# Layer-norm statistics on another engine in a hybrid decoder trunk: ScalarE's accumulators in place of VectorE's batch-norm instructions

## The chip, the core and the metric

The kernel runs on one core of a Trainium2 chip. A core has TensorE (PE, matmuls and transpositions; PEld is its weight load), VectorE (DVE), ScalarE (ACT), GpSimd (POOL) and SyncE (SP, which here only issues DMAs). Each engine works through its own queue in order; semaphores let an instruction wait for another engine or for a DMA. The metric is the device time of one execution in microseconds; of several executions the median is taken.

## The reference

One decoder layer on 1024 positions of 1024 features. The normalised input is projected to four parts; three mixers work on them, one of which is the spatial gating unit that this change touches:

```
h = rms_norm(x, g_mix)
z_a, z_b, z_u, z_v = split(h @ w_in)            # 384, 256, 384, 384 columns
y_a = s5_mixer(z_a, ...)                        # diagonal state space model, a scan
y_b = pool_mixer(z_b, ...)
# spatial gating unit
u = gelu(z_u);  v = gelu(z_v)
mu  = mean(v);  var = mean((v - mu)^2)          # over the 384 columns
v = (v - mu) * rsqrt(var + eps) * ln_g + ln_b
y_c = u * (tril(w_spatial) @ v per head and chunk of 128 + b_spatial)
x = x + concat(y_a, y_b, y_c) @ w_out
x = x + (silu(h2 @ w_gate) * (h2 @ w_up)) @ w_down,   h2 = rms_norm(x, g_ffn)
return rms_norm(x, g_final)
```

## The kernel before

Everything is float32. A matrix product is made of three products of the float32r type: each operand is split into a hi part (a cast) and a lo part (the rest), and `mm3` (L320 to L324) issues hi x hi, hi x lo and lo x hi into the same PSUM tile. The casts are ScalarE's, the subtractions for the lo parts mostly VectorE's.

The work goes in stages. First x is scaled, split and multiplied for z_a, the input of the state space model; z_a is scaled by 1/rms (`zf`, L400), stored to a DRAM buffer `zdram` and loaded back in another order as `u` (`load_u`, L420; half of these loads are issued from ACT's queue, half from SP's). Meanwhile VectorE and GpSimd compute the parameters of the state space model (`ssm_params`, `csquare`). Then the steps of the string `SEQ = '0v1woBu2uuup'` are written out: a scan block (`0`, `1`, `2`), the two halves of the z_v work (`v`, `w`), the z_b product (`B`), pairs of z_u tiles (`u`) and others. Output projection, feed-forward part (by far the longest, with a Strassen-like scheme) and the final norm follow.

A scan block calls `state_in` (L257): VectorE (in one block GpSimd for a part) builds `wp` by three instructions (L264 to L266), TensorE transposes it in eight pieces of 128 x 128 into two PSUM tiles (`wtr`, L270) and ScalarE copies these out as `wt` (L271). With `wt` and `u` TensorE computes the scan's input (`x`, L450). Rotation tables (`tables`, L288 to L294), a swap of halves by DMA, the scan itself (L458) and another swap follow.

`z_v(b)` (L529 to L562) handles four of the eight position tiles, b = 0 or 1. For each tile 24 matmuls of 384 columns fill a PSUM tile `zv` (tag `pm`, four buffers), ScalarE applies the gelu into `v` (L542), VectorE takes the statistics (`bn_stats`, `bn_aggr`, L543 and L544, mean and variance into `mv`). After four tiles VectorE computes the reciprocal root (`rsqrt`, three Newton steps on 128 x 4, L93 to L100), scales `v` by two instructions per tile (L549, L550), ScalarE casts hi parts and VectorE or GpSimd subtracts for three lo parts `vhl` (L554, L555; which engine is read from `ENG['vl']`, one digit for each, 1 for GpSimd). Six spatial products `sp` follow (L322 to L324), evacuated by ScalarE as `mx` (L562).

What order the instructions get in each engine's queue is not the order of the text. The Tile framework schedules at build time against its own simulated time (`schedule_with_timeline_sim=True`): of the instructions that are ready it takes those written earlier first, and a `high_priority` block, such as the one around `zf`, goes ahead. `behind(first, *later)` (L57) adds an edge by which each later instruction is queued after the first one on its engine; it makes no semaphore wait. In the kernel before, one such edge puts eight broadcasting matmuls (`spread`) behind the first z_v tile.

Of the kernel before, what the change touches and what calls it, by code (L numbers as in the profile page):

```python
# [10 lines left out]
F32 = mybir.dt.float32  # L11
F32R = mybir.dt.float32r
I32 = mybir.dt.int32
AF = mybir.ActivationFunctionType
# [3 lines left out]
P = 128  # L18
# [10 lines left out]
EPS = 1e-6  # L29
# [4 lines left out]
SEQ2 = 'aVYqYYAGb'  # L34
KA = [int(c) for c in '567']
KB = [k for k in (3, 4, 0, 1, 2, 5, 6, 7) if k not in KA]
ENG = dict(e.split(":") for e in 'sq:0,wq:001,tc:101,ts:010,m1:101,m2:001,ps:01010,vl:100,ln:0,wl:0,wo:0,vq:000,vv:111,vs:000,t1:0000,t2:0110,T2:0010,T3:0010,T4:0000,gs:1111,fl:0001,cq:0,pw:1,gz:0001,rs:0000,dg:0,am:00,fg:1000,fa:0011'.split(","))
NVT = 2
NWARM = 11
NTAIL = 4  # L40
# [3 lines left out]
def trunk(ctx: ExitStack, tc: tile.TileContext, A, O):  # L44
    nc = tc.nc
    V, S, GP, PE, SY = nc.vector, nc.scalar, nc.gpsimd, nc.tensor, nc.sync
    mult, add, sub = ALU.mult, ALU.add, ALU.subtract

    def en(key, i=0, default="0"):
        v = ENG.get(key, default)  # L50
        return GP if v[i % len(v)] == "1" else V

    def behind(first, *later):

        for i in later:
            tc.add_manual_dep(i.ins, first.ins.name, mybir.DependencyInfo(mybir.DependencyClass.NoSync, mybir.DependencyReason.DATA), reason="order")
# [4 lines left out]
    kst = scK.enter_context(tc.tile_pool(name="kst", bufs=1, side="right"))  # L61
# [8 lines left out]
    def slot(shape, dt, name):  # L70
        return s4.tile(shape, dt, tag="s4", name=name)

    def slot5(shape, dt, name):
        return s5.tile(shape, dt, tag="s5", name=name)


    ident = const.tile([P, P], F32, tag="ident", name="ident")
# [10 lines left out]
    def rsqrt(dst, src, shape, pool, eng):  # L88

        bits = pool.tile(shape, I32, tag="rs_i", name="rs_i", bufs=2)  # L90
        t = pool.tile(shape, F32, tag="rs_t", name="rs_t", bufs=2)
        vh = pool.tile(shape, F32, tag="rs_v", name="rs_v", bufs=2)
        V.tensor_scalar(bits, src.bitcast(I32), -0.5, float(0x5F3759DF), mult, add)  # L93
        eng.tensor_scalar(vh, src, -0.5, None, mult)
        y = bits.bitcast(F32)
        for it in range(3):
            eng.tensor_tensor(t, y, y, mult)
            eng.tensor_tensor(t, t, vh, mult)
            o = dst if it == 2 else y
            eng.scalar_tensor_tensor(o, t, 1.5, y, add, mult)  # L100
# [77 lines left out]
    pw = kst.tile([P, 2, 9, G], F32, tag="pw", name="pw")  # L178
# [70 lines left out]
        e.tensor_tensor(o, d, n.unsqueeze(1).to_broadcast([P, 2, G]), mult)  # L249

    G8 = 8

    def state_in(i):

        wp, wq = slot5([P, G8, L, CH], F32, f"wp{i}"), slot5([P, G8, L, CH], F32, f"wq{i}")
        w = slot5([P, G8, P], F32, f"wt{i}")
        gs = slice(i * G8, (i + 1) * G8)  # L257

        def bb(t):
            return t[:, gs].unsqueeze(2).to_broadcast([P, G8, L, CH])  # L260

        def bw(t):
            return t[:, 0:8, gs].rearrange("p t g -> p g t").unsqueeze(3).to_broadcast([P, G8, L, CH])
        V.tensor_tensor(wp, bb(bq[:, 0]), bw(pw_r), mult)  # L264
        en('wq', i).tensor_tensor(wq, bb(bq[:, 1]), bw(pw_is), mult)
        V.tensor_tensor(wp, wp, wq, add)  # L266
        for q in range(2):
            pw = py(f"wtr{i}{q}")
            for g in range(4):
                PE.transpose(pw[:, g * P:(g + 1) * P], wp[:, q * 4 + g].rearrange("p s c -> p (s c)"), ident)  # L270
            S.copy(w[:, q * 4:q * 4 + 4], pw.rearrange("p (g m) -> p g m", g=4))  # L271
        return w

    def tables(i):

        c, s = slot5([P, G8, P], F32, f"tabc{i}"), slot5([P, G8, P], F32, f"tabs{i}")
        tb = slot5([P, 2, G8, 64], F32, f"tbt{i}")
# [22 lines left out]
    def xs(hl, k, c):  # L300
        return xhl[k // 4][:, hl, k % 4, c]

    psA = ExitStack()
    ps = psA.enter_context(tc.tile_pool(name="ps", bufs=1, space=PSUM))

    def pm(name, shape=(P, 512)):
        return ps.tile(list(shape), F32, tag="pm", name=name, bufs=4)

    def py(name, shape=(P, 512)):
        return ps.tile(list(shape), F32, tag="py", name=name, bufs=2)  # L310

    def px(name, shape=(P, 512)):
        return ps.tile(list(shape), F32, tag="px", name=name, bufs=2)
# [6 lines left out]
    def mm3(out, lh, ll, rh, rl, start, stop, more=False):  # L320

        PE.matmul(out, lh, rh, start=start, stop=False, skip_group_check=more)  # L322
        PE.matmul(out, lh, rl, start=False, stop=False, skip_group_check=more)  # L323
        return PE.matmul(out, ll, rh, start=False, stop=stop, skip_group_check=more)  # L324

    def load_w(k, c0, n, e, eh=S):

        raw = pa.tile([P, 384], F32, tag="wraw", name=f"wraw{c0}_{k}", bufs=3)
        SY.dma_start(raw[:, :n], A["w_in"][k * P:(k + 1) * P, c0:c0 + n])
        w = pa.tile([P, 2, 384], F32R, tag="w3", name=f"w{c0}_{k}", bufs=8)  # L330
        (S.copy if eh is S else eh.tensor_copy)(w[:, 0, :n], raw[:, :n])
        e.tensor_tensor(w[:, 1, :n], raw[:, :n], w[:, 0, :n], sub)
        return w
# [11 lines left out]
    for k in range(KD):  # L345
# [15 lines left out]
        else:  # L361
            sq = slot5([P, NT], F32, f"sq{k}")
# [13 lines left out]
    with tc.high_priority():  # L376
# [5 lines left out]
        rstd = kst.tile([P, 8], F32, tag="rstd", name="rstd")  # L382
# [3 lines left out]
        dg = slot([P, 8, P], F32, "dg")  # L386
# [22 lines left out]
    e = V  # L409
# [111 lines left out]

    lngb = pv.tile([P, 2, 384], F32, tag="lngb", name="lngb")
    S.dma_start(lngb, A["lngb"])
    st6 = kst.tile([P, 8, 6], F32, tag="st6", name="st6")
    mv = kst.tile([P, 8, 2], F32, tag="mv", name="mv")
    lrs = kst.tile([P, 8], F32, tag="lrs", name="lrs")
    wv, wu, mx = [], [], []

    def z_v(b):  # L529
        if not wv:  # L530
            wv.extend(load_w(k, 1024, 384, en('wl', k, '1')) for k in range(KD))
        bs = slice(4 * b, 4 * b + 4)
        vt = pv.tile([P, 4, 384], F32, tag="vt", name=f"vt{b}", bufs=NVT)
        for n in range(4 * b, 4 * b + 4):
            pz = pm(f"zv{n}")
            c = slice(n * P, (n + 1) * P)
            for k in range(KD):
                last = mm3(pz[:, 0:384], xs(0, k, c), xs(1, k, c), wv[k][:, 0], wv[k][:, 1], k == 0, k == KD - 1)
            if n == 0:
                behind(last, *spread)  # L540
            v = vt[:, n % 4]
            S.activation(v, pz[:, 0:384], AF.Gelu_apprx_tanh, scale=rstd[:, n:n + 1])  # L542
            V.bn_stats(st6[:, n], v)  # L543
            V.bn_aggr(mv[:, n], st6[:, n])  # L544
        V.tensor_scalar(lrs[:, bs], mv[:, bs, 1], EPS, None, add)
        rsqrt(lrs[:, bs], lrs[:, bs], [P, 4], const, V)
        for n in range(4 * b, 4 * b + 4):
            v = vt[:, n % 4]
            V.scalar_tensor_tensor(v, v, mv[:, n, 0:1], lngb[:, 0], sub, mult)  # L549
            V.scalar_tensor_tensor(v, v, lrs[:, n:n + 1], lngb[:, 1], mult, add)  # L550
        vhl = [slot([P, 2, 4, P], F32R, f"vhl{b}{i}") for i in range(3)]
        for i in range(3):
            v = vt[:, :, i * P:(i + 1) * P]
            S.copy(vhl[i][:, 0], v)  # L554
            en('vl', i).tensor_tensor(vhl[i][:, 1], v, vhl[i][:, 0], sub)  # L555
        if not mx:
            mx.extend(slot([P, 8, P], F32, f"mx{i}") for i in range(3))
        for h in range(6):
            pz = px(f"sp{h}{b}")
            c = slice((h % 2) * 64, (h % 2) * 64 + 64)  # L560
            mm3(pz[:, 0:256], wsh[:, h], wsl[:, h], vhl[h // 2][:, 0, :, c], vhl[h // 2][:, 1, :, c], True, True)
            S.activation(mx[h // 2][:, bs, c], pz[:, 0:256].rearrange("p (n d) -> p n d", n=4), AF.Identity, bias=bsp[:, h:h + 1])  # L562
# [104 lines left out]
    vv = bigS[:, 0:3456].rearrange("p (g t c) -> p g t c", g=G, t=9)  # L667
    tt = bigS[:, 3456:6528].rearrange("p (g m) -> p g m", g=G)
    vq = bigS[:, 6528:6528 + 1152].rearrange("p (g t c) -> p g t c", g=G8, t=9)
# [482 lines left out]
    def final_lo():  # L1152
# [5 lines left out]
        for n in range(4):  # L1158
            o, rn = uu[n], r[:, n:n + 1]
            for h in range(2):  # L1160
                if ENG.get("fl", "0011")[n] == "1":
                    S.activation(o[:, h], cs[0, h][:, n], AF.Copy, scale=rn)
# [34 lines left out]
    for v in range(len(SLOTS)):  # L1197
        i, p = place[v]
# [43 lines left out]
    for i in ORDER:  # L1242
        pz = [pd.tile([P, 512], F32, tag="pd", name=f"q{i}{n}") for n in range(4)]
# [4 lines left out]
        for q, n in order:  # L1248
# [7 lines left out]
            c = slice(n * P, (n + 1) * P)  # L1256
# [67 lines left out]
```

## Time and profile before

| what | value |
|---|---|
| median of 3 runs | 991.65 us (990.21 to 992.48) |
| the profiled execution | 991.64 us |
| its span, first to last instruction | 989.6 us |
| mean granted TensorE clock | 0.976 |
| busy PE / PEld / DVE / ACT / POOL | 931.4 / 777.9 / 708.7 / 386.0 / 126.7 us |

The profile gives, for that execution, busy times of the engines over the span and in any stretch of it, the instructions in order of time, groups of instructions by line, and who waited for whom. A row of the timeline reads: start, duration, engine, line of the kernel, operation, output<-inputs, shapes, and in brackets the idle time of the engine before it with what ended it. A releaser is inferred from semaphores; where the engine named had long been done, it was another. A row of waits reads: engine and line that waited, releaser, total us, number of times, longest. TensorE is the busiest engine (94% of the span), but the stage of the change lies between 43 and 125 us, where the other engines have to be looked at.

### The profile page before, as it was taken

The page shows a single profiled execution, that of the slowest core. Times are in us where ns is not written, and L with a number is a line of the kernel's source. Part 1 is how long each engine was busy: PE and PEld are TensorE (multiplying, and loading weights), DVE is VectorE, ACT ScalarE, POOL GpSimd, SP SyncE. Part 2 cuts the span into 40 slices and gives each one's busy share as a digit, 9 for nine tenths or more (in the row PEclk, how much of TensorE's full clock was granted, in tenths as well). Part 3 has the DMA queues.
Part 4 walks back from the last instruction along what each step waited for, and adds up shares of the span by engine and source line. Part 5 has one row for each costly group of instructions (what it writes and reads, how often), then busy time and mean ns, then how long its engine had stood idle before and what let it go on. Part 6 is the DMA issues. An engine that isn't in the chain of part 4 may idle for free. (4 is left out here: it accounts for less than half of the span.)

```text
span 989.6 us, 12459 instructions
## 1 busy us (share of the span) xinstructions
PE 931.4 (94%) x4312; PEld 777.9 (79%) x4312; DVE 708.7 (72%) x1291; ACT 386.0 (39%) x646; POOL 126.7 (13%) x147
## 2 busy tenths in 40 slices
PE   9988898687899889999999999999999999999996
PEld 7888698466688678888888888888888788888885
DVE  7999998992466988666675675685683755655786
ACT  7524242113463544333333333333333354333543
POOL 0236625611200000000000000000002100000031
PEclk9999999987999989999999999999999999999998
DMA  7233334435332015543544434535427999862013
GB/s 271 89 102 70 99 83 107 124 74 104 116 128 85 33 35 169 192 169 138 174 149 167 168 129 170 176 121 180 173 94 266 397 386 387 297 215 83 0 43 128
DMA packets 89599, 150.77 MB, mean 152 GB/s; under 512 B 11728, under 2 KB 42720, under 8 KB 89536
## 3 DMA queue, kind: packets, MB, share of 16 engines
q1 hardware_dynamic: 71136, 119.50, 36.0%
q10 hardware_dynamic: 17040, 26.02, 8.5%
q0 software_dynamic: 1360, 4.46, 1.3%
q8 instruction: 34, 0.56, 0.2%
q14 instruction: 29, 0.24, 0.1%
HBM read 104.23 MB, written 41.68 MB: 147 GB/s over the span
## 5 line engine op out<-in xcount | busy, mean ns | idle before, releaser
L1143 DVE TENSOR_TENSOR ol<-d,oh 128x1024 fp32r<-128x1024 f32 x77 | 95.7, 1258 | 70.2 <-PE q L324 52.5
L323 PE MATMUL q<-ol,oh 128*128 128x512 f32 x308 | 119.8, 390 | 2.2 <-DVE ol L1143 2.2
L1142 ACT CAST oh<-d 128x1024 fp32r<-128x1024 f32 x77 | 80.5, 1053 | 103.5 <-PE q L324 88.9
L324 PE MATMUL q<-oh,ol 128*128 128x512 f32 x308 | 119.7, 389 | 0.0
L322 PE MATMUL q<-oh 128*128 128x512 f32 x308 | 113.1, 389 | 0.0
L323 PEld LDWEIGHTS q<-ol,oh 128*128 128x128 f32 x308 | 57.8, 188 | 14.6 <-DVE ol L1143 2.6
L322 PE MATMUL X<-bb,S 128*128 128x512 f32 x176 | 68.7, 391 | 0.2 <-ACT bb L826 0.2
L323 PE MATMUL X<-bb,S 128*128 128x512 f32 x176 | 68.6, 390 | 0.0
L324 PE MATMUL X<-bb,S 128*128 128x512 f32 x176 | 68.6, 390 | 0.0
L324 PEld LDWEIGHTS q<-oh,ol 128*128 128x128 f32 x308 | 57.8, 188 | 12.1
L322 PEld LDWEIGHTS q<-oh 128*128 128x128 f32 x308 | 57.8, 188 | 11.9
L886 ACT CAST S<-r 128x512 fp32r<-128x512 f32 x66 | 39.9, 621 | 64.2 <-PE X L324 54.7
L774 POOL DMA_DIRECT2D td<-tx x3 | 1.9, 636 | 469.8 <-DVE tx L766 469.8
L323 PE MATMUL wo<-wo,yT 128*128 128x512 f32 x128 | 51.3, 402 | 7.7 <-DVE wo L601 7.7
L322 PE MATMUL wo<-wo,yT 128*128 128x512 f32 x128 | 51.0, 408 | 3.1 <-DVE x L644 3.1
L324 PE MATMUL wo<-wo,yT 128*128 128x512 f32 x128 | 50.3, 401 | 0.0
L887 DVE TENSOR_TENSOR S<-r,S 128x512 fp32r<-128x512 f32 x66 | 44.5, 689 | 1.7 <-ACT S L886 1.2
L943 DVE TENSOR_TENSOR c<-X,c 128x512 f32<-128x512 f32 x20 | 13.8, 691 | 41.0 <-PE X L324 41.0
L943 DVE TENSOR_TENSOR c<-y,c 128x512 f32<-128x512 f32 x28 | 19.3, 691 | 29.8 <-PE y L324 29.8
L322 PE MATMUL y<-T,S 128*128 128x512 f32 x104 | 40.6, 390 | 0.0
L324 PE MATMUL y<-T,S 128*128 128x512 f32 x104 | 40.5, 389 | 0.0
L323 PE MATMUL y<-T,S 128*128 128x512 f32 x104 | 40.5, 389 | 0.0
(381 smaller groups left out, 2363.2 us busy)
## 6 DMA issues: line engine op xcount, KB each, us to landing
r<-in_w_gu SPq DMA_DIRECT2D x44, 512.0 KB, 4.5
d<-actd SPq DMA_DIRECT2D x77, 256.0 KB, 5.4
actd<-c ACTq DMA_DIRECT2D x30, 512.0 KB, 3.0
d<-td SPq DMA_DIRECT2D x44, 256.0 KB, 5.4
t<-in_w_down SPq DMA_DIRECT2D x40, 256.0 KB, 3.4
d<-in_w_down SPq DMA_DIRECT2D x33, 256.0 KB, 5.5
td<-t SPq DMA_DIRECT2D x19, 256.0 KB, 3.6
wraw<-in_w_in SPq DMA_DIRECT2D x24, 192.0 KB, 2.7
```

Of the source, the lines that this page charges most:

```text
L322: PE.matmul(out, lh, rh, start=start, stop=False, skip_group_check=more)
L323: PE.matmul(out, lh, rl, start=False, stop=False, skip_group_check=more)
L324: return PE.matmul(out, ll, rh, start=False, stop=stop, skip_group_check=more)
L774: i = e.dma_start(d, t)
L886: S.copy(hi, src)
L887: V.tensor_tensor(lo, src, hi, sub)
L943: o.last = V.tensor_tensor(t, pz, t, add)
L1142: S.copy(h, tv)
L1143: t = V.tensor_tensor(l, tv, h, sub)
```

## The change

```
-ENG = dict(... 'vl:100' ...)
+ENG = dict(... 'vl:000' ...)
...
+    wtr = []
...
-                PE.transpose(pw[:, g * P:(g + 1) * P], wp[:, q * 4 + g].rearrange("p s c -> p (s c)"), ident)
+                wtr.append(PE.transpose(pw[:, g * P:(g + 1) * P], wp[:, q * 4 + g].rearrange("p s c -> p (s c)"), ident))
...
-    st6 = kst.tile([P, 8, 6], F32, tag="st6", name="st6")
...
             if n == 0:
                 behind(last, *spread)
+            elif n == 2:
+                behind(last, *wtr[0:8])
             v = vt[:, n % 4]
-            S.activation(v, pz[:, 0:384], AF.Gelu_apprx_tanh, scale=rstd[:, n:n + 1])
-            V.bn_stats(st6[:, n], v)
-            V.bn_aggr(mv[:, n], st6[:, n])
-        V.tensor_scalar(lrs[:, bs], mv[:, bs, 1], EPS, None, add)
+
+            S.activation(v, pz[:, 0:384], AF.Gelu_apprx_tanh, scale=rstd[:, n:n + 1], accum_out=mv[:, n, 0:1])
+            V.tensor_scalar(mv[:, n, 0:1], mv[:, n, 0:1], -1.0 / 384, None, mult)
+            S.activation(pz[:, 0:384], v, AF.Square, bias=mv[:, n, 0:1], accum_out=mv[:, n, 1:2])
+        V.tensor_scalar(lrs[:, bs], mv[:, bs, 1], 1.0 / 384, EPS, mult, add)
         rsqrt(lrs[:, bs], lrs[:, bs], [P, 4], const, V)
         for n in range(4 * b, 4 * b + 4):
             v = vt[:, n % 4]
-            V.scalar_tensor_tensor(v, v, mv[:, n, 0:1], lngb[:, 0], sub, mult)
+            V.scalar_tensor_tensor(v, v, mv[:, n, 0:1], lngb[:, 0], add, mult)
             V.scalar_tensor_tensor(v, v, lrs[:, n:n + 1], lngb[:, 1], mult, add)
```

Three things change. The gelu's instruction also sums its output over the 384 columns into `mv[:, n, 0]`; VectorE turns the sum into minus the mean by an instruction on one column; and ScalarE makes a second pass, the square of v minus the mean, with its sum in `mv[:, n, 1]`. The squares themselves are written over the PSUM tile that the gelu has read, and are not used. The factor 1/384 of the variance goes into the instruction that adds eps. Second, all three lo parts of each half are VectorE's, where the first was GpSimd's. Third, an edge keeps the eight transpositions of the first scan block's weights behind the last matmul of the third z_v tile (n = 2) on TensorE's queue.

More of the change, by code (lines that the diff above doesn't have):

```diff
@@ L36 @@
 KB = [k for k in (3, 4, 0, 1, 2, 5, 6, 7) if k not in KA]
-ENG = dict(e.split(":") for e in 'sq:0,wq:001,tc:101,ts:010,m1:101,m2:001,ps:01010,vl:100,ln:0,wl:0,wo:0,vq:000,vv:111,vs:000,t1:0000,t2:0110,T2:0010,T3:0010,T4:0000,gs:1111,fl:0001,cq:0,pw:1,gz:0001,rs:0000,dg:0,am:00,fg:1000,fa:0011'.split(","))
+ENG = dict(e.split(":") for e in 'sq:0,wq:001,tc:101,ts:010,m1:101,m2:001,ps:01010,vl:000,ln:0,wl:0,wo:0,vq:000,vv:111,vs:000,t1:0000,t2:0110,T2:0010,T3:0010,T4:0000,gs:1111,fl:0001,cq:0,pw:1,gz:0001,rs:0000,dg:0,am:00,fg:1000,fa:0011'.split(","))
 NVT = 2
```

## The prediction

> **What bounds the kernel.** I read the page first, then the busy time by stretch, the waits of TensorE (PE), and last the timelines of VectorE (DVE), ScalarE (ACT) and GpSimd (POOL) around the z_v tiles. In the stretches the columns are stretch, its length, and busy time with the number of instructions of each engine.
>
> ```profile
> span 989.6 us, 12459 instructions
> 43.00:66.00 23.00, 22.41 (x135) 22.09 (x133) 22.93 (x58) 7.59 (x11) 13.88 (x18) 1.00 0.26 93
> 66.00:90.00 24.00, 19.60 (x119) 19.42 (x120) 23.97 (x78) 9.38 (x20) 12.93 (x18) 0.93 0.42 66
> 90.00:120.00 30.00, 24.12 (x113) 19.12 (x113) 30.00 (x67) 6.87 (x15) 17.77 (x27) 0.99 0.33 95
> 345.00:720.00 375.00, 369.96 (x1651) 306.49 (x1652) 257.52 (x429) 137.34 (x228) 0.00 (x0) 0.99 0.45 154
> ```
>
> Over most of the span PE is the bound (369.96 of 375 us). The edits lie elsewhere, between 43 and 125 us, and there DVE is busy 22.93 of 23, 23.97 of 24 and 30.00 of 30 us, while PE is idle 4.4 us in the second stretch and 5.9 in the third. ACT works 7.59 + 9.38 + 6.87 = 23.8 of 77 us.
>
> ```profile
> PE wtr L270 <- ACT vt L542: 3.1, 1, 3.1
> PE wtr L270 <- DVE wp L266: 1.9, 1, 1.9
> PE zb L324 <- DVE w L332: 1.5, 1, 1.5
> PE sp L322 <- ACT vhl L554: 4.4, 1, 4.4
> ```
>
> These are PE's long waits there, and all four end at DVE. The first row names ACT, but the timeline shows another releaser:
>
> ```profile
> 62.85 0.54 DVE L543 BATCH_NORM_STATS2 st<-vt 128x6 f32<-128x384 f32 x1
> 63.32 0.18 DVE L240 TENSOR_TENSOR q_s<-ecs 128x48 f32<-128x48 f32 x1
> 63.52 0.17 DVE L544 BATCH_NORM_AGGREGATE mv<-st 128x2 f32<-128x6 f32 x1
> 63.61 0.14 DVE L246 TENSOR_TENSOR q_d<-q_s 128x24 f32<-128x24 f32 x1
> 63.77 0.60 DVE L549 SCALAR_TENSOR_TENSOR vt<-vt,mv,lngb 128x384 f32<-128x384 f32 x1
> 64.38 1.21 DVE L264 TENSOR_TENSOR wp<-bq,pw 128x1024 f32<-128x1024 f32 x1
> 66.77 0.55 DVE L543 BATCH_NORM_STATS2 st<-vt 128x6 f32<-128x384 f32 x1
> 67.24 1.20 DVE L266 TENSOR_TENSOR wp<-wp,wq 128x1024 f32<-128x1024 f32 x1
> 68.54 1.94 PE L270 MATMUL wtr<-ident,wp 128*128 128x128 f32 x8 [3.12 <-ACT vt L542]
> ```
>
> DVE finishes wp at 67.24 + 1.20 = 68.44 and PE turns it at 68.54. The fourth wait ends likewise: DVE writes the last scaled v tile (L550), ACT casts it, and PE starts at 119.22.
>
> ```profile
> 116.85 1.67 DVE L550 SCALAR_TENSOR_TENSOR vt<-vt,lrs,lngb 128x384 f32<-128x384 f32 x3
> 119.22 0.80 PE L322 MATMUL sp<-vhl,wsh 128*128 128x256 f32 x2 [4.42 <-ACT vhl L554]
> ```
>
> So until about 119 us the time is set by DVE's queue, and what leaves that queue counts.
>
> **The statistics.** Eight BATCH_NORM_STATS2 and eight BATCH_NORM_AGGREGATE leave DVE, all before 98 us:
>
> ```profile
> L543 DVE BATCH_NORM_STATS2 st<-vt x8: 521/546/554, 51.8 to 95.8; 128x6 f32<-128x384 f32 x8
> 70.14 0.16 DVE L545 TENSOR_SCALAR lrs<-mv 128x4 f32<-128x4 f32 x1
> 70.21 0.61 DVE L549 SCALAR_TENSOR_TENSOR vt<-vt,mv,lngb 128x384 f32<-128x384 f32 x1
> ```
>
> What one costs a full queue is the time from its start to the next start: 63.32 - 62.85 = 0.47 and 63.61 - 63.52 = 0.09 us. Eight of each are 3.8 + 0.7 = 4.5 us. Added are eight TENSOR_SCALAR on one column. The nearest row, on four columns, lasts 0.16 but lets the next begin after 0.07, so they cost 0.6 us, with 1.3 as the other end. The subtraction that becomes an addition (L549) costs nothing: same instruction, same operands.
>
> ACT takes over with an accumulator on Gelu and a second pass, Square.
>
> ```profile
> L1150 ACT ACTIVATE junk<-c x16: 622/632/634, 830.1 to 981.6; 128x512 f32<-128x512 f32 x16
> L1150 ACT ACTIVATION_READ_ACCUMULATOR junk<-c x16: 183/187/191, 830.7 to 982.1; 128x1 f32 x16
> L807 ACT ACTIVATE jk<-x x32: 411/417/418, 283.9 to 330.5; 128x256 bf16<-128x256 f32 x32
> ```
>
> Square with an accumulator takes 0.417 us on 256 columns and 0.632 on 512, so about 0.52 on 384, and each accumulator is read out by an instruction of 0.187. A tile adds 0.52 + 2 x 0.19 = 0.9 us, eight tiles 7.2 us, beside 23.8 busy of 77. Its throughput is covered. Square also keeps the PSUM tile it overwrites, but there are four of these:
>
> ```profile
> 42.00:66.00 24.00, 20.87 (x118) 20.44 (x118) 1.75 (x3) 1.00 0.25 89
> ```
>
> Of the z_v tiles alone PE ran 118 matmuls in 20.87 us, 0.177 each, or 4.2 us for the 24 of a tile. The bank is wanted again three tiles, 12.7 us, later.
>
> What isn't in the trace is the new round trip: Gelu, DVE's division, Square, and back to DVE, which may write v only once Square has read it, and needs the variance of four tiles for its reciprocal root. DVE's queue is full of other work, so the lower end is nothing; the upper end is one Square and read (0.7 us) laid bare at the end of each of the two batches, 1.4. I take 1.0, nearer the upper end because the queue is in order: a late Square holds everything behind it, the scan and the split of w_in included.
>
> **The split by VectorE alone.** In each batch one of three lo parts moves from POOL to DVE.
>
> ```profile
> 79.22 1.34 POOL L555 TENSOR_TENSOR vhl<-vt,vhl 128x512 fp32r<-128x512 f32 x1
> 79.32 1.78 DVE L555 TENSOR_TENSOR vhl<-vt,vhl 128x512 fp32r<-128x512 f32 x1
> 81.50 0.68 DVE L555 TENSOR_TENSOR vhl<-vt,vhl 128x512 fp32r<-128x512 f32 x1
> 119.24 2.75 POOL L555 TENSOR_TENSOR vhl<-vt,vhl 128x512 fp32r<-128x512 f32 x1 [3.40 <-ACT vhl L554]
> ```
>
> In the first batch the DVE split that began beside POOL's took 1.78 us, and the one after it 0.68. POOL's held it back by 1.10. Taking it over costs 0.68 and may give 1.10 back: -0.4, or +0.7 if another POOL instruction takes the place. I take -0.4. In the second batch POOL's split takes 2.75 us where DVE needs 0.68, but it begins when PE has already started: from -0.3 to +0.7, and I take nothing, as a shorter part on a fuller queue.
>
> The Trainium skill, page "SBUF — State Buffer", section "Who interferes with whom", says that a DVE instruction with two SBUF inputs and a GpSimd instruction that reads SBUF exclude each other for a whole instruction. The first pair agrees: 1.78 against 0.68 us.
>
> **The transpositions.** The edge asks that the eight transpositions of wp stand behind 3 x 24 = 72 matmuls of z_v. The row above has them behind 118. In this order the edge binds nothing and costs nothing; what it costs if they do move is a rival.
>
> **The sum.** At 118 us DVE is ahead by 4.5 - 0.6 + 0.4 - 1.0 = 3.3 us, so PE starts at about 116 instead of 119.22. PE's own arrival there moves about as much, because its wait before that follows DVE too, and seven of the eight statistics lie ahead of it (the seventh, and the wait):
>
> ```profile
> 92.48 0.55 DVE L543 BATCH_NORM_STATS2 st<-vt 128x6 f32<-128x384 f32 x1
> 93.41 0.50 PE L324 MATMUL zb<-xhl,w 128*128 128x512 f32 x1 [1.46 <-DVE w L332]
> ```
>
> So the wait itself stays near 4.4. Behind it the DVE-paced work to 230 us and the PE-bound stages keep the lead, as each DMA there is released by work that is itself earlier. The profiled execution took 991.64, of which 2.04 are outside its span, and the median of the runs is 991.65: 991.6 - 3.3 = 988.3 us. About 0.2%, 2.0 us, is what a measurement of this kernel can tell from no change.
>
> **Rivals.** *The clock comes back as well.* The eighth column of these stretches is the granted clock, and after the long wait it is low:
>
> ```profile
> 119.00:126.00 7.00, 6.46 (x18) 4.92 (x18) 7.00 (x12) 5.80 (x12) 2.75 (x1) 0.51 0.32 88
> 126.00:132.00 6.00, 6.00 (x39) 5.89 (x38) 6.00 (x9) 2.76 (x7) 2.44 (x1) 1.00 0.60 130
> ```
>
> PE's 6.46 us at a clock of 0.51 would be 3.3 at full clock: 3.2 are lost. The second stretch, with the wait of 3.1 us, has 0.93, the third, with the waits of 1.9 and 1.5 before or in it, 0.99. If DVE's second batch gains some 1.5 us more than PE's arrival, the wait falls below 3 us and the loss goes: 988.3 - 3.2 = 985.1. Against it, arrival and release hang on the same queue.
> The Trainium skill, page "TensorE: Matmul & The Clock Gate", Part 1, puts half rate behind an idle window of about 3.4 us; 4.42 us agrees, and the 0.93 beside 3.1 us says that a little less can do. By the rule the sum stays at 988.3 while the wait is 4.4, and is 985.1 if it drops under 3.4.
>
> *The gain is eaten on the way.* If the scheduler, finding DVE freer, sets the transpositions straight behind the third z_v tile, PE meets them at the tile's end, shown by the Gelu that it releases:
>
> ```profile
> 57.48 0.58 ACT L542 ACTIVATE vt<-zv,rstd 128x384 f32<-128x384 f32 x1 [0.27 <-PE zv L324]
> 63.61 3.46 ACTq L420 DMA_DIRECT2D u<-zdram  x4
> 67.12 0.58 ACT L542 ACTIVATE vt<-zv,rstd 128x384 f32<-128x384 f32 x1 [9.06 <-DMA zdram<-zf]
> ```
>
> wp would be ready at about 67, so PE idles 9.5 us instead of 3.1, 6.4 more, and the later waits of 1.9 and 1.5 absorb 3.4. It then reaches sp about 3 us late, at 118, and starts there 1 to 2 us earlier than now: about 990.2, no change that shows.
>
> *Slower: the second Square behind a DMA.* ACT stands still from 58.1 to 67.12 for the landing of zdram ahead of its u loads. If Square of the second tile, whose mean DVE can only give after 62.9, is queued behind those loads, it ends near 68. DVE's L549 of that tile stands ahead of wp (63.77 before 64.38), so DVE idles some 4.8 us and wp comes at about 72: +4.8 - 3.3 = +1.5, and a PE wait of over 7 us with slow matmuls behind it adds 1 to 2: about 994.3. It decides only if both orders hold; against it, the mean comes before zdram lands, so a scheduler that takes what is ready puts Square first.
>
> *A table switch at each Square.* The load before the first Gelu takes 1.28 us; sixteen would be 20.5 on ACT, more than its slack beside the 9 us standstill, and cost 5 to 10 us: about 999.
>
> ```profile
> 47.26 1.28 ACT L542 ACT_TABLE_LOAD   x1 [1.72 <-DVE rstd L100]
> 261.66 1.28 ACT L739 ACT_TABLE_LOAD   x1
> ```
>
> Against it: L807's Squares from 283.9 us follow the sigmoid load with none of their own. The Trainium skill, "ScalarE: Activation LUTs", section "Table sets: the hidden batching unit", prices a switch to another set at about 2.66 us, yet holds that cheap functions are in every set; the second half is what the trace shows.
>
> **Chances.** The sum as worked out 0.45, the clock as well 0.19, eaten 0.19, Square behind the DMA 0.14, table switches 0.03. Faster is 0.64, same 0.19, slower 0.17. The range runs from 983.5 (the clock case with the unknown round trip at nothing and a microsecond more of POOL contention gone) to 994.3; outside it lie the tables and the tails of a new instruction order, together under 0.2.
>
> **What would show it.** Right: no L543 or L544, per z_v tile two ACTIVATE and two accumulator reads, no new table load, no L555 on POOL; the first wtr wait under 2 us, sp's first matmul of the second batch at 115 to 117, and the same lead at 345 us. Wrong: DVE idle with ACT's Square as releaser, transpositions at 57 us, or the lead gone by 230 us in another collision of DVE and POOL.

## The result, and the profile after

The changed kernel takes 1002.68 us (median of 4 runs, 1001.12 to 1004.23), the kernel before 991.36 in the runs beside it: a ratio of 1.0112, 95% interval 1.0096 to 1.0129. It is slower by 11.3 us; the forecast was 988.3 us and the range ended at 994.3. The profiled execution took 1004.23 us, with a span of 1002.3, a mean granted clock of 0.969, and PE / DVE / ACT / POOL busy 933.6 / 706.7 / 391.5 / 124.9 us. DVE's sum fell by only 2.0 us: 5.7 us of statistics left it, 1.1 us of small divisions and 0.8 us of splits came to it, and others of its instructions took longer. One execution of b2 (1560.58 us, at a granted clock of 0.556) and one of c2 (1077.63 us, at 0.835) fell in a slow state and are left out of the figures below.

Busy time by stretch of the changed kernel, in the columns of the prediction's first fence:

```profile
43.00:66.00 23.00, 22.64 (x136) 22.27 (x134) 22.76 (x63) 9.08 (x18) 13.75 (x19) 1.00 0.24 86
66.00:90.00 24.00, 20.73 (x124) 20.28 (x125) 23.93 (x71) 11.17 (x30) 12.90 (x18) 0.93 0.45 72
90.00:120.00 30.00, 24.77 (x115) 19.32 (x113) 27.78 (x64) 9.58 (x21) 17.22 (x24) 1.00 0.42 113
126.00:132.00 6.00, 6.00 (x23) 6.00 (x22) 6.00 (x15) 1.15 (x3) 0.00 (x0) 0.57 0.24 67
180.00:230.00 50.00, 36.57 (x150) 25.86 (x150) 44.33 (x52) 8.45 (x19) 16.28 (x10) 0.83 0.32 82
230.00:285.00 55.00, 39.51 (x219) 33.62 (x217) 17.64 (x21) 20.86 (x30) 11.53 (x9) 0.88 0.45 103
```

The same view of the kernel before, for the two stretches that the prediction did not show:

```profile
180.00:230.00 50.00, 39.41 (x190) 29.35 (x190) 44.57 (x51) 11.76 (x24) 17.38 (x12) 0.93 0.37 82
230.00:285.00 55.00, 45.45 (x223) 37.99 (x223) 24.97 (x32) 25.35 (x38) 9.28 (x7) 0.88 0.45 118
```

Up to 90 us the rows moved little, apart from ACT's added work. Between 90 and 120 DVE has 2.2 us of air that it did not have, 2.00 of it in one wait for the DMA of a swap, ahead of 108.4 us. But between 180 and 285 us, where no line was edited, PE works 36.57 + 39.51 = 76.1 us instead of 84.9. PE's long waits in the changed kernel, from 40 to 300 us:

```profile
PE wo L324 <- DVE wo L604: 8.3, 1, 8.3
PE wo L323 <- DVE x L647: 6.3, 2, 4.2
PE sp L323 <- ACT vhl L557: 6.3, 1, 6.3
PE y L711 <- DMA u<-zdram: 3.8, 1, 3.8
PE gt L718 <- ACT yg L714: 3.3, 1, 3.3
PE wtr L271 <- ACT zv L547: 3.2, 1, 3.2
PE zb L325 <- DVE w L333: 2.2, 2, 1.3
```

and those of the kernel before that answer to the new ones (the waits for yc are left out; they come to 4.8 us in both):

```profile
PE wo L323 <- DVE wo L601: 7.7, 1, 7.7
PE wo L322 <- DVE x L644: 3.1, 3, 1.5
PE y L708 <- DMA u<-zdram: 2.3, 1, 2.3
PE gt L715 <- ACT yg L711: 1.7, 1, 1.7
```

The wait ahead of the second sp batch grew from 4.4 to 6.3 us instead of staying. Four rows of the changed kernel's timeline, on three engines:

```profile
63.72 0.58 ACT L547 ACTIVATE zv<-vt,mv 128x384 f32<-128x384 f32 x1 [5.06 <-DVE mv L546]
67.55 1.22 DVE L267 TENSOR_TENSOR wp<-wp,wq 128x1024 f32<-128x1024 f32 x1
68.87 1.16 PE L271 MATMUL wtr<-ident,wp 128*128 128x128 f32 x8 [3.23 <-ACT zv L547]
123.35 0.80 PE L323 MATMUL sp<-vhl,wsh 128*128 128x256 f32 x2 [6.25 <-ACT vhl L557]
```

The transpositions come at 68.87 instead of 68.54, still at the end of wp (67.55 + 1.22), and sp at 123.35 instead of 119.22. Yet the last z_u matmul starts at 169.7 instead of 169.0, so nearly all of this had been caught up by then, z_b having run ahead of sp. The loss must arise later.

The queues tell more. They are no longer the queues of the kernel before with the edits put in. Compared by operation and tile, the order differs in more than a hundred places on DVE and on PE, in dozens on ACT and in a few on SP and POOL, all of them ahead of the feed-forward part. No queue was ordered by hand, but for the one edge: the scheduler, given other instructions, chose another order. One place where this shows, in the kernel before:

```profile
206.74 1.35 DVE L683 TENSOR_TENSOR bigS<-parC,pw 128x1152 f32<-128x1152 f32 x1
209.11 1.35 DVE L684 TENSOR_TENSOR bigS<-bigS 128x1152 f32<-128x1152 f32 x1
210.49 1.05 ACT L693 COPY bigS<-k 16x512 f32<-16x512 f32 x2
215.95 4.44 ACTq L696 DMA_DIRECT2D bigS<-bigS  x4
```

and in the changed one:

```profile
212.26 1.29 DVE L647 TENSOR_TENSOR x<-wo,x 128x512 f32<-128x512 f32 x2 [2.31 <-PE wo L325]
213.47 1.35 DVE L686 TENSOR_TENSOR bigS<-parC,pw 128x1152 f32<-128x1152 f32 x1
217.53 1.35 DVE L687 TENSOR_TENSOR bigS<-bigS 128x1152 f32<-128x1152 f32 x1
218.91 1.05 ACT L696 COPY bigS<-k 16x512 f32<-16x512 f32 x2 [4.57 <-DVE bigS L687]
225.90 4.58 ACTq L699 DMA_DIRECT2D bigS<-bigS  x4
```

The third pair of weight products of the state space model now stands behind two accumulations of x that wait for PE. ScalarE's k copies write over the space that these products read, so they come 8.4 us later, and the DMAs that build the operand of y start 9.95 us later.

### The profile page after: what moved, and what is told of

Same layout as the page of the kernel before. It is cut to its first block, busy times and chain, and to the rows that moved or that the text cites. A ratio compares the mean times of both kernels' runs of the same rounds, so it can differ in the third digit from the quotient of the medians.

```text
span 1002.3 us, 12483 instructions
## 1 busy us (share of the span) xinstructions
PE 933.6 (93%) x4312; PEld 780.1 (78%) x4312; DVE 706.7 (71%) x1285; ACT 391.5 (39%) x670; POOL 124.9 (12%) x145
## 5 line engine op out<-in xcount | busy, mean ns | idle before, releaser
L324 PE MATMUL wo<-wo,yT 128*128 128x512 f32 x128 | 52.2, 409 | 8.3 <-DVE wo L604 8.3
L323 PE MATMUL wo<-wo,yT 128*128 128x512 f32 x128 | 51.3, 411 | 6.4 <-DVE x L647 6.3
L325 PE MATMUL wo<-wo,yT 128*128 128x512 f32 x128 | 51.4, 409 | 2.0 <-DVE yT L585 2.0
L769 DVE TENSOR_TENSOR tx<-t,t 128x256 f32<-128x256 f32 x22 | 9.2, 420 | 45.9 <-DMA t<-in_w_down 45.9
```

The costliest lines, as they stand in the source:

```text
L769: o.sum = V.tensor_tensor(o.x, r0[:, 1], r1[:, 1], add), V.tensor_tensor(r0[:, 1], r0[:, 1], r0[:, 0], add)
```

## The experiments

Three theories. **A**: the edits cost little themselves; the 11 us come from the other sequence that the scheduler chose. **B**: the statistics on ScalarE cost directly, by their round trips. **C**: the split by VectorE is the cost. To part instructions from sequence, a list of instruction numbers per engine is put into the kernel, and a chain of edges that only fix the order in the queue and make no wait:

```
+PIN = [[int(n) for n in q.split()] for q in (
...
+    made = {i.name: i for i in nc.cur_bb.bb.instructions}
+    for queue in ([n for n in q if f"I-{n}" in made] for q in PIN):
+        for n, m in zip(queue, queue[1:]):
+            tc.add_manual_dep(made[f"I-{m}"], f"I-{n}", mybir.DependencyInfo(mybir.DependencyClass.NoSync, mybir.DependencyReason.DATA), reason="order")
```

Line numbers in the kernels with such lists are 7 or 8 higher than in the kernels that they are made from.

**a1: the edits in the sequence of before.** The changed kernel with the chain above, its lists taken from the kernel before.

> This kernel has all the edits of the changed one, but every engine's queue up to the feed-forward part is held, by order-only edges that make no wait, in the sequence that the kernel before has; a ScalarE Square and its small division stand where the batch-norm instructions stood. Theory A (the edits themselves cost little, and the 11 us arise between 180 and 285 us from the different sequence that the build-time scheduler chose): k and y start near 205 and 227 us as before, and the time is 986 to 992 us. Theory B (the statistics on ScalarE cost directly: a later sp at 123 us, a PE wait of 6 us, carried to the end): sp still starts near 123 us and the time is 998 us or more. Theory C (the split by VectorE alone is the cost) also gives 995 or more.

Measured: 994.5 us (10 runs, 990.25 to 995.46), ratio 1.0030 (1.0014 to 1.0046). Between the theories: the old sequence takes away 8 of the 11 us, but 3 remain, and they are local. The timeline of a1, on ACT and PE:

```profile
90.95 0.58 ACT L554 ACTIVATE zv<-vt,mv 128x384 f32<-128x384 f32 x1 [4.28 <-DVE mv L553]
91.72 0.80 PE L330 MATMUL zb<-xhl,w 128*128 128x512 f32 x1 [2.39 <-ACT zv L554]
95.57 0.58 ACT L554 ACTIVATE zv<-vt,mv 128x384 f32<-128x384 f32 x1
96.32 0.80 PE L330 MATMUL zb<-xhl,w 128*128 128x512 f32 x1 [3.39 <-ACT zv L554]
```

z_b needs the PSUM tiles of z_v as soon as z_v has ended, and a Square that has still to write into one holds it. The two Squares start 6 and 9 us after the ends of their gelus (84.8 and 86.6 us), since the mean waits its turn in DVE's queue. In three of the ten executions the time was 990.3 to 991.2, in the others 993 to 995.5; the traced one took 994.75. What sets the three apart is open.

**b1: a1 with Square writing elsewhere.**

```
+    sqj = kst.tile([P, 384], mybir.dt.uint8, tag="sqj", name="sqj")
...
-            S.activation(pz[:, 0:384], v, AF.Square, bias=mv[:, n, 0:1], accum_out=mv[:, n, 1:2])
+            S.activation(sqj, v, AF.Square, bias=mv[:, n, 0:1], accum_out=mv[:, n, 1:2])
```

> The edits held in the sequence of the kernel before, as in a1, with one difference: Square writes its unused squares into a small tile of SBUF of its own (one byte per element), so that a z_v tile of PSUM is free when the gelu has read it. In a1 TensorE's z_b waited 5.8 us at 89 to 96 us for Squares, and the clock of the stretch 90 to 120 us was 0.83. If the held PSUM tile is what costs a1 its 3.4 us: no z_b wait for ScalarE's Square, clock 0.95 or more in 90 to 120, the last z_u near 167 to 169 us (a1: 171.1) and 987 to 991 us. If the cost is the round trip itself (in-order queues of ScalarE and VectorE, whatever Square writes): the last z_u stays at 170 or later and the time at 993 to 996 us.

Measured: 988.15 us (10 runs, 987.21 to 990.42), ratio 0.9960 (0.9945 to 0.9974). Its timeline:

```profile
91.23 0.62 ACT L555 ACTIVATE sqj<-vt,mv 128x384 uint8<-128x384 f32 x1 [3.87 <-DVE mv L554]
96.03 0.61 ACT L555 ACTIVATE sqj<-vt,mv 128x384 uint8<-128x384 f32 x1
117.52 0.79 PE L330 MATMUL sp<-vhl,wsh 128*128 128x256 f32 x2 [4.36 <-ACT vhl L565]
```

The Squares stand where they stood in a1, as late as there, but z_b waits 1.0 us in all, for a split of its weights, and none of it for ScalarE. So the held PSUM tile, not the round trip, cost a1 its time, and without it the edits gain.

**a2: the instructions of before in the sequence of the changed kernel.** The kernel before, with the lists of the changed one.

> The instructions of the kernel before (batch-norm statistics on VectorE, the first lo part on GpSimd), with every engine's queue up to the feed-forward part held in the sequence of the changed kernel. Theory A (the sequence costs, not the instructions): 999 to 1004 us, with k first at about 209 and glu last at about 289 us. Theory B (statistics on ScalarE cost directly): 989 to 993 us. A time between, 994 to 998, would mean that both share.

Measured: 1003.77 us (4 runs, 1002.74 to 1004.60), ratio 1.0129 (1.0108 to 1.0151). None of the edited instructions is in it, and it is as slow as the changed kernel. This settles A for the 11 us, and theory B is out as their cause.

**a3 and a4: one edit alone, in the scheduler's own sequence.** a3 has the statistics, with the split's digit put back and no edge; a4 has the split alone.

```
a3  'vl:100' kept, no behind(last, *wtr[0:8])
a4  -'vl:100'  +'vl:000', bn_stats and bn_aggr kept
```

> The statistics by ScalarE alone; the first lo part stays GpSimd's, and there is no edge for the transpositions. The scheduler chooses its own sequence, which differs from both others. Theory A: the loss depends on where the scheduler then puts the state weights' DMAs and the k copies, anywhere from 988 to 1004. Theory B: 998 or more whatever the sequence. Theory C (the split): about 991.

> The split by VectorE alone, with the batch-norm statistics of the kernel before and no edge. Theory B (statistics): 989 to 993 us. Theory C (the split is the cost): 998 or more. Theory A: the sequence changes here too, so anything from 988 to 1002, and the traces show it between 180 and 285 us.

Measured: a3 989.06 us (986.45 to 990.60), ratio 0.9976 (0.9963 to 0.9989); a4 995.18 us (993.41 to 997.20), 1.0041 (1.0026 to 1.0056). Alone, one edit gains 0.24% and the other loses 0.41%; together they lose 1.12%. Such parts do not add up, and neither B nor C explains both. That a4 loses by its own sequence is likely, since in the sequence of before the split alone moves nothing that can be told (b1 and c3 below), but a4's sequence was not tried with other instructions. The edge alone was not run either: it asks for 72 matmuls ahead of the transpositions where the kernel before has 118, so it need not move anything there, but that it moves nothing is not shown.

**b4: the instructions of before in a3's sequence.** The kernel before with the lists of a3.

> The instructions of the kernel before (batch-norm statistics) held in the sequence of a3, the kernel with the statistics by ScalarE alone that was 2 us faster than before. If a3 gained by its sequence: 986 to 990 us. If it gained by what leaves VectorE (my sum for the statistics gave 2.9 us): 991 to 994 us, 2 to 4 above a3.

Measured: 991.88 us (989.83 to 995.45), ratio 1.0004 (0.9989 to 1.0019). a3 is 0.28% faster in the same sequence, so it is its instructions that gain, 2.8 us, though the two intervals touch. The traces agree: the last z_u matmul starts at 172.7 us in b4 and at 169.9 in a3.

**c2, c3, c4: the rest of the table.** c2 is the changed kernel with b1's edit of Square, c3 is b1 with `vl:100`, c4 is a3 with b1's edit of Square and a free sequence.

> The changed kernel as it is, but Square writes into a small SBUF tile, as in b1; the scheduler then gives the same sequence as for the changed kernel. In that sequence no long wait of TensorE ends with a Square, so if the held PSUM tile costs only where z_b meets it: 1000 to 1003 us, no change. If the held tile is part of the loss of the changed kernel too: 994 to 998 us.

> b1 without the second edit: the first lo part of each half is GpSimd's again, everything else as in b1 (sequence of the kernel before, Square into SBUF). The prediction priced the split at -0.4 us in the first half and nothing in the second; by that this kernel takes 988 to 989 us, up to 0.5 above b1. If the split by VectorE costs time on its full queue: 986 to 987. If it gains more, through the collision with GpSimd: 990 to 991.

> The statistics by ScalarE alone, Square into SBUF, and the sequence that the scheduler itself chooses for it, nearly that of a3 (which took 989.06). If Squares hold up TensorE in that sequence as in a1, this gains up to 3 us: 985 to 988 us. If they don't (a3 shows no z_b wait for a Square): 988 to 990 us, as a3.

Measured: c2 999.86 us, ratio 1.0089 (1.0059 to 1.0120), not told apart from the changed kernel; c3 988.55 us, 0.9984 (0.9967 to 1.0000); c4 988.94 us, 0.9976 (0.9961 to 0.9992), not told apart from a3. Ratios to the kernel before, by sequence and instructions:

| sequence | instructions of before | edits, Square over PSUM | edits, Square to SBUF |
|---|---|---|---|
| of before | 1 | 1.0030 (a1) | 0.9960 (b1), 0.9984 without the split (c3) |
| of the changed kernel | 1.0129 (a2) | 1.0112 (the changed kernel) | 1.0089 (c2) |
| of a3, without the split | 1.0004 (b4) | 0.9976 (a3) | 0.9976 (c4) |

The columns hold the same instructions, the rows the same sequence (c4's own differs from a3's in a few places on PE and POOL). Down a column the ratio moves by more than 1%; along a row by 0.7% at most, and in the middle row the edits seem to gain too, though there the intervals overlap.

**b2 and b3: which part of the sequence.** b2 is the changed kernel with the sequence of before held from 172 us on; b3 is the kernel before with the changed kernel's from 172 us on.

> The changed kernel with its own sequence up to about 172 us and the sequence of the kernel before held from there to the feed-forward part. If the loss of 11 us is made by the sequence behind 172 us: z_u ends near 170 as in the changed kernel, k begins near 205, and the time is 990 to 994 us. If it comes from the statistics, or from the sequence ahead of 172 us and only shows later: 998 us or more.

> The counterpart: the kernel before, whose first 172 us keep their own sequence, with the sequence of the changed kernel held from there on. If the sequence behind 172 us makes the loss: 998 to 1003 us, with the last k at 233 us or later. If it is made ahead of 172 us: 990 to 993 us.

Measured: b2 991.23 us, ratio 0.9995 (0.9975 to 1.0014); b3 999.35 us, 1.0070 (1.0047 to 1.0093). So the sequence behind 172 us costs 7 to 12 us, whichever instructions stand ahead of it. The first matmul of y, by the groups of that tile in the kernel before, the changed one, b2 and b3:

```profile
L708 PE MATMUL y<-bigS,u x24: 272/275/422, 227.4 to 244.7; 128*128 128x128 f32 x24
```

```profile
L711 PE MATMUL y<-bigS,u x16: 275/275/377, 235.1 to 238.4; 128*128 128x128 f32 x16
```

```profile
L718 PE MATMUL y<-bigS,u x20: 270/275/417, 228.4 to 244.7; 128*128 128x128 f32 x20
```

```profile
L715 PE MATMUL y<-bigS,u x16: 275/275/377, 233.5 to 236.8; 128*128 128x128 f32 x16
```

With the old sequence behind 172 us y starts at 227.4 to 228.4, with the new one at 233.5 to 235.1.

**c1, d1, d2: where in it.** c1 and d2 keep the changed kernel's sequence and move the k chain of the result section ahead; in c1 also ScalarE's casts and SP's loads of w_out, which had been put between its parts, move behind it. d1 takes the sequence of before from 203 us on.

```
c1  DVE: third pair of bigS products ahead of x<-wo101, x<-wo111
    PE: k02, k10 ahead of wo141
    ACT: casts of oraw3_0, oraw4_0, oraw0_0 behind the last k copy
    SP: second bigS DMAs ahead of oraw0_0
d2  the moves on DVE and PE alone
```

> The changed kernel in its own sequence, with one group of instructions put back to where the kernel before has it: VectorE's third pair of weight products (the multiplication and the subtraction of bigS for i = 2) ahead of two accumulations of x, TensorE's k products of the third and fourth PSUM tile ahead of nine output products, ScalarE's last k copies and the second bigS DMAs ahead of casts and loads of w_out. Theory A in its narrow form (the loss behind 172 us is this chain: product, k copy, bigS DMA, y): ScalarE's first k copies at about 213 us instead of 218.9, first bigS DMAs near 219 instead of 225.9, y near 229 to 230 instead of 235.1, and 995 to 998 us. If the loss is spread over the whole sequence from 172 us on: 1000 us or more. Nothing is changed ahead of 205 us, so about 3 us of the loss must stay.

> As c1, but only VectorE's third pair of weight products and TensorE's k products of the third and fourth tile are moved; the casts and loads of w_out stay in the places of the changed kernel. In c1 y came at 229.9 instead of 235.1, but ScalarE's yg then made TensorE wait 8.3 us, since a cast of w_out put ahead of it waited for its load. If that wait was made by my own move of the cast: here y near 231 us, gt waits 3 to 4 us, and 996 to 999 us. If the early y always meets a late yg: 999 to 1001 us.

> The changed kernel in its own sequence up to about 203 us, and from there to the feed-forward part in the sequence of the kernel before (b2 did the same from 172 us and took 991.4). If the loss lies mainly in the chain behind 203 us (third weight product, k copies, bigS DMAs, and the w_out loads and casts set among them): 993 to 996 us, y near 230 us, glu last near 282. If it lies mainly between 172 and 203 us: 998 us or more.

Measured: c1 999.68 us, ratio 1.0094 (1.0070 to 1.0118): the expectation was missed. y came at 229.9 us as expected, but then the waits of c1 show

```profile
PE gt L725 <- ACT yg L721: 8.3, 1, 8.3
```

where the changed kernel has 3.3: the cast that I had moved ahead of yg waits 8.76 us for its load. d2, without that move, has 3.3 there, y at 230.8 us and 998.84 us, ratio 1.0070 (1.0057 to 1.0083). So two moved groups on two queues give back about 4 of the 11 us, shown. d1 gives 996.78 us, 1.0064 (1.0044 to 1.0084), a little above what was expected: behind 203 us lie about 5 of the 11. That leaves some 5 between 172 and 203 us by the medians of b2 and d1. Their traces do not show these: the profiled executions took 994.32 and 994.41 us, the highest of b2's nine and the lowest of d1's four. What makes that second part is open.

**d3: the collision at 190 us.** b1, with GpSimd's products of `s5_weights` given to VectorE.

```
-'vv:111'
+'vv:000'
```

> b1, with the three products of s5_weights that are GpSimd's (6.6 us of POOL at 192 to 199 us) given to VectorE, each right ahead of its subtraction. In all kernels here VectorE takes 9.5 us for two subtractions of w_out that need 0.7 each, while GpSimd runs these products, and TensorE waits 7.7 us for them. If that is a collision of the two engines over SBUF: the wo subtractions take 1.4 us, TensorE's wait falls below 3 us, VectorE gets 4 us more work, and the time is 983 to 986 us. If the wait is set by something else (the loads of w_out): 988 us or more, as b1.

Measured: 986.07 us (6 runs, 983.42 to 989.97), ratio 0.9942 (0.9923 to 0.9961), the lowest of all and at the edge of what was expected; its interval overlaps b1's, so the gain over b1 is not shown. The traced execution is the fastest of the six. In b1, first the two rows of DVE in which the subtractions lie, by time and by group, then POOL:

```profile
190.49 9.50 DVE L612 TENSOR_TENSOR wo<-oraw,wo 128x512 fp32r<-128x512 f32 x2
L612 DVE TENSOR_TENSOR wo<-oraw,wo x16: 678/685/8894, 127.0 to 298.8; 128x512 fp32r<-128x512 f32 x16
190.00 1.00 POOL L697 TENSOR_TENSOR dsk<-dsk,ident 16x384 f32<-16x384 f32 x1
190.97 6.64 POOL L693 TENSOR_TENSOR bigS<-parC,pw 128x1152 f32<-128x1152 f32 x3
197.58 1.25 POOL L522 TENSOR_TENSOR phl<-pw,phl 128x512 fp32r<-128x512 f32 x1
```

In d3:

```profile
190.20 1.29 DVE L612 TENSOR_TENSOR wo<-oraw,wo 128x512 fp32r<-128x512 f32 x2 [0.36 <-ACT wo L611]
```

The two subtractions take 1.29 instead of 9.50 us, and PE's wait of 7.7 us for them is gone. The second row gives shortest, median and longest in ns: one subtraction lasted 8.89 us, where most take 0.69. Part of the gain is lost to waits for x behind DVE's added work, 5.2 us between 180 and 300 us where b1 has 1.7.

## Why the prediction was wrong, step by step

The step that failed is "Behind it the DVE-paced work to 230 us and the PE-bound stages keep the lead". It rests on an assumption: every term of the sum was set into the order of before, and the text took it that the order stays. "In this order the edge binds nothing" may be true; but the order was not this one any more. a2 shows that the new order was worth 12.8 us (1.29%), four times the whole sum. Two of the rivals moved single instructions, the transpositions and one Square; a new order as a whole was named only at the end of the part on chances, among tails under 0.2.

A second step failed too: the PSUM tile that Square holds, which the sum put at nothing. The kernel that the sum describes, the edits in the order of before, is a1, and a1 is 0.30% slower, 3.0 us, where the sum gave a gain of 3.3.

The size of the rest was nearly right. With Square moved out of PSUM and the order of before, b1 gains 0.40% of 991.57, 4.0 us by the ratio, and c3 0.16%, 1.6 us; in a3's order it is 2.8. Of the steps:

- **Statistics leave DVE** (3.9 us net): they left, but the changed kernel's queue did not run ahead by it. The scheduler set three more steps of the scan's swaps (L463 at 112.29, L454 at 117.97 and L455 at 120.37, some 1.2 us each) ahead of the last scalings of v, and DVE waited 2.00 us for a swap's DMA, up to 108.4, so sp came at 123.35. In the order of before (b1) it came at 117.52, where the forecast said about 116, behind a wait of 4.36, where it said 4.4.
- **ACT's work** (0.9 us per tile): nearly right; Square took 0.586 us where 0.52 was estimated. The group rows of the changed kernel for Square are

```profile
L547 ACT ACTIVATE zv<-vt,mv x8: 582/586/587, 52.2 to 98.0; 128x384 f32<-128x384 f32 x8
L547 ACT ACTIVATION_READ_ACCUMULATOR zv<-vt,mv x8: 186/187/189, 52.7 to 98.5; 128x1 f32 x8
```

so a tile adds 0.586 + 2 x 0.19 = 0.97 us. The trace has the one table load ahead of the first gelu, and none at a Square.
- **"Square also keeps the PSUM tile it overwrites, but there are four of these"**: failed in the order of before. The estimate counted the next z_v tile. After the last one z_b takes the same four buffers, and the Squares of the last two tiles come late. It cost 0.70% between a1 and b1, 6 us by the medians (994.5 and 988.15), more than the gain itself. In the changed kernel's own order the same edit of Square (c2) gives nothing that can be told.
- **The round trip** (1.0 us, 0 to 1.4): not seen by itself; b1 holds it and still gains.
- **The split** (-0.4 us): b1 and c3 differ by 0.4 us of median, and their intervals overlap. Not told apart from nothing, as said.
- **The clock**: the wait that grew to 6.25 us was followed by a granted clock of 0.57 in 126 to 132 us, where before had 1.00. But before had 0.51 in 119 to 126 us, where the changed kernel has 0.64: the slow stretch came later, and z_u ended only 0.7 us later than before. The rival's condition, a wait below 3 us, was met in a3 and b4 (0.6 and 0.9 us at sp), and the clock was 1.00 from 119 to 132 us there. In 90 to 120 us, though, it was 0.94 and 0.89 instead of 0.99, and b4's time is that of the kernel before: that the 3.2 us come back is not shown.
- **The lead is kept**: it was not. In the changed kernel's own sequence, a2 (instructions of before) and the changed kernel, last z_u matmuls:

```profile
L331 PE MATMUL zu<-w,xhl x64: 333/337/522, 130.0 to 173.1; 128*128 128x384 f32 x64
```

```profile
L325 PE MATMUL zu<-w,xhl x64: 336/336/522, 126.2 to 169.7; 128*128 128x384 f32 x64
```

The edits bring 3.4 us here, almost the forecast, though this compares two single executions. At the end 1.1 us is left in the medians (1003.77 and 1002.68), which the intervals do not tell apart. Where the rest goes was not tried.

Of the rivals, the second Square behind a DMA did not happen (Square of the second tile at 63.72 stands ahead of the u loads), nor did the transpositions at 57 us. The sign "the lead gone by 230 us in another collision of DVE and POOL" hit the place by luck: the collision is in the kernel before as well, 7.7 us of PE's time and 8.3 in the changed kernel, so it makes at most 0.6 us of the loss. The Trainium skill, page "SBUF — State Buffer", section "Who interferes with whom", says that a DVE instruction with two SBUF inputs and one of GpSimd that reads SBUF exclude each other. d3 agrees: 9.50 us beside GpSimd's products, 1.29 without. The lower end of the range, 983.5, does not come out of its own terms (985.1 - 1.0 - 1.0 = 983.1); nothing hangs on it.

## What to carry to other kernels

When a scheduler writes the queues, an edit is two changes: its instructions and a new order; the second was the larger here, 11 to 13 us against 3, and a sum over instructions set into the old order does not show it. Price the edit in the old order, then hold the order by edges and measure both parts apart; if the pinned edit gains and the free one loses, keep the pin or move the few instructions that fell behind. A scratch output written over a PSUM tile was not free in a1: ask which tile is wanted next under the same tag, the next stage's as well.

## What was not expected of the hardware

A 128x512 subtraction that mostly takes 0.69 us took 8.89 us on DVE in b1, while POOL ran five instructions one behind the other from 190.00 to 198.83 us: DVE got no turn between POOL's instructions, not merely a slower one. In the changed kernel one took 9.03 us. And Square with its accumulator cost nearly the same whether it wrote f32 over PSUM (0.586 us) or one byte per element into SBUF (0.615).
